# One ordered TensorE stretch per expert in a routed mixture of experts, with the row scatter split between weight tiles

## The chip, the cores and the metric

The kernel runs on one core of a Trainium2 chip. The metric is the device time of one execution in microseconds (us), as the median of several executions. Profiled numbers come from one execution recorded by the hardware profiler. Its span runs from the first to the last recorded instruction, and its own time is a little longer than the span.

## The reference

The reference is one encoder layer on 256 tokens of width 1024: an input projection, three token mixers (latent attention, a state-space scan, a convolution module), gates and an output projection, a layer norm, then a mixture of experts and a second layer norm. The change lies in the mixture of experts alone:

```
logits = t @ router_w + router_b
top_vals, top_idx = top_k(logits, 4)          # 4 of 32 experts per token
gates = softmax(top_vals)
for each expert e, for its tokens x:
    h = x @ w_gu[e] + b_gu[e]                 # 1024 -> 2048
    gate, up = min(h[:, :1024], 7), clip(h[:, 1024:], -7, 7)
    y = ((up + 1) * gate * sigmoid(1.702 * gate)) @ w_dn[e] + b_dn[e]
    out[tokens] += gates * y
x = layernorm(2 ** 0.25 * x + out)
```

All matrices are float32. The weights of one expert are 12.6 MB, those of all experts 402.7 MB, and each is read from HBM once.

## The kernel before

The mixer part comes first and takes some 400 us. The rest of the time is a loop over the 32 experts, written out in full.

**Weights.** Each expert has 12 tiles of 1 MB: 8 of the up projection (one for each 128 rows of the input width) and 4 of the down projection. They go through a ring of 19 tiles (`load`, line 721). SyncE issues the transfers in order, and each waits until TensorE has read the tile that was in that place 19 loads before. The first 19 tiles are loaded while the mixers still run.

**Two forms of an expert.** How many tokens an expert has is known only at run time. A form with 64 token slots (`many`) runs when the expert has more than 32 tokens, and a form with 32 slots (`four`) when it has at most 32, or more than 64; with more than 64 tokens (`over`) both run, and the second form takes the tokens from 65 on. Each piece is a conditional block: `on(cond, pe_part, other_part)` on line 1179 puts the first part under a branch on TensorE's queue and the second under a branch on ScalarE's and VectorE's queues. The flags come from memory into registers (line 1171). Where a block isn't taken, the queue jumps over it and raises the block's semaphores in its place. In the profiled execution 19 experts run `four` alone, 10 run `many` alone and 3 run both (counted from the matmuls of lines 1217 and 1227 in the table below).

**An expert** (`expert`, line 1168):
- `gather_more` (line 1195) for `over` alone: 32 small matmuls fetch the further tokens, into PSUM bank 1, and ScalarE and VectorE copy them out.
- The up projection in four pairs of weight tiles (`up_many`, `up_four`, lines 1210 and 1220), the `many` block and the `four` block of each pair one after the other.
- `swiglu_into` (line 1084) on VectorE and ScalarE.
- `turn_many` and `turn_four` (lines 1249 and 1263): matmuls of one column that bring the tokens' gates into slot order (`gate_mm`), for `many` also a broadcast of the expert's row of token ranks (`pbr`), the bias of the down projection, and transposes of the activations. Then VectorE copies the gates to SBUF (`gsl`, lines 1258 and 1272), builds the 0/1 scatter matrix `sc` from the ranks (`slots`, line 1099), and ScalarE copies the transposes to `hT`.
- The down projection (lines 1278 and 1286), and `weigh` (line 1141): ScalarE and VectorE multiply by the gates and split the result in two terms, `yh` and `yl`.
- For `over`, a scatter of the first form's rows into the sum (`pom`, line 1296).
- For `four`, a second broadcast of the ranks into `pb2` (line 1298), `slots` and `weigh`.

**Two pieces belong to the neighbours.** `flush(prev)` (line 1156) scatters the previous expert's rows: for each half `c` of the 256 tokens, four matmuls into two PSUM banks, then two VectorE adds into the sum `acc` (its tile bears the name `xn` in the profile). `fill` (line 1390) prepares the tokens of the next pair of experts: in an even expert it gathers them (8 matmuls of 512 columns, `pgx`, then two copies), in an odd expert it transposes them (`spread_rows`, line 973: 8 transposes, `pgt`, then 8 copies that ScalarE and VectorE take in turn from the same two banks). In the code `first` and `second` stand after the first pair of up tiles and after the activation.

**What sets the order.** The tile framework orders the instructions of each engine by a simulation, except inside `tc.manual_schedule`, which keeps the order of the code for the engines that it names. Here `pe_order()` (line 1312) encloses each piece by itself, so that the framework may place the pieces of TensorE against each other. In the trace it places both `flush` and `fill` between two experts: after an expert's last matmul of the down projection come the skipped blocks, `pbs` (that is `pb2`), then `pgt` and `pos` (`fill`, `flush`) or `pos` and `pgx`, and only then the next expert's bias and up projection.

**PSUM** has 8 banks: five fixed ones, `bank(0)` to `bank(4)`, and three that rotate under the name `sm`, which `flush`, `fill`, the gates, the ranks and `pom` share.

At the last expert (line 1404) `flush` comes ahead of a branch over a large block for experts with more than 96 tokens, which isn't taken.

Of the kernel before, what the change touches and what calls it, by code (L numbers as in the profile page):

```python
# [18 lines left out]
P = 128  # L19
# [158 lines left out]
def tile_trunk(ctx, tc, xT_d, xn_d, wf_d, vec_d, row_d, rw_d, cst_d, cst2_d, rope_d, ln1_d, ln2_d,  # L178
# [895 lines left out]
    def sm(name, shape=None):  # L1074
        return pse.tile(shape or [P, 512], F32, tag="sm", name=name, bufs=3)
# [16 lines left out]
    def gate_mm(pgs, lhs, e):  # L1092
        for c in range(2):
            l = lhs(c).bitcast(F32)
            n = l.shape[-1]
            for h in range(P // n):
                T.matmul(pgs[h * n:(h + 1) * n, 0:1], l, Gm[c][:, e:e + 1], start=(c == 0), stop=(c == 1))
# [27 lines left out]
    def gate_slots(lhs, e, name):  # L1125
# [6 lines left out]
        gsl = ex.tile([P, 1], F32, tag="gsl", name=f"gsl{name}", bufs=4)  # L1132
# [23 lines left out]
    def flush(prev):  # L1156
        if prev:
            e, sc, yh, yl = prev
            for c in range(2):
# [8 lines left out]
    def expert(e, oh, xg, bl, wt, prev, cur, fill):  # L1168
# [8 lines left out]
        first, second = (fill, lambda: flush(prev)) if e % 2 else (lambda: flush(prev), fill)  # L1177

        def on(cond, *parts):

            for c_, f in zip(cond, parts):
                if f:
                    with tc.If(c_):  # L1183
                        with pe_order():
                            f()
# [7 lines left out]
        pg = bank(1, f"pgs{e}", [P, KT, TINY])  # L1193
# [36 lines left out]
        for k0 in range(0, KT, 2):  # L1230
            on(many, lambda: up_many(k0))
            on(four, lambda: up_four(k0))
            if k0 == 0:
                with pe_order():
                    first()
# [4 lines left out]
        with pe_order():  # L1240
            second()
        pY = [bank(i, f"pY{e}{i}") for i in range(2)]
        pgL, pgS, pbr = [sm(f"pgs{e}{i}") for i in range(3)]
# [3 lines left out]
        gsl = [ex.tile([P, 1], F32, tag="gsl", name=f"gsl{e}{i}", bufs=4) for i in range(2)]  # L1247

        def turn_many():
            gate_mm(pgL, lambda c: oh[:, c, e % 2], e)  # L1250
            T.matmul(pbr[:, 0:S], idr[:, e:e + 1].to_broadcast([P, P]), rankT, start=True, stop=True)
# [5 lines left out]
        def turned_many():  # L1257
            V.tensor_copy(gsl[0], pgL[:, 0:1])
            slots(sc, pbr, 0, e)
# [3 lines left out]
        def turn_four():  # L1263
            gate_mm(pgS, lambda c: ohs[:, c], e)
# [6 lines left out]
        def turned_four():  # L1271
            V.tensor_copy(gsl[1], pgS[:, 0:1])
# [20 lines left out]
        on(many, None, lambda: weigh(pY[0], gsl[0], yh, yl))  # L1293
        for c in range(2):
            pos = [sm(f"pom{e}{c}{n}") for n in range(2)]
            on(over, lambda: scatter(pos, c, sc, (yh, yl)), lambda: [add(c, n, pos[n]) for n in range(2)])
        pb2 = sm(f"pbs{e}", [P, S])
        on(four, lambda: T.matmul(pb2, idr[:, e:e + 1].to_broadcast([P, P]), rankT, start=True, stop=True),  # L1298
           lambda: (slots(sc, pb2, 1, e), weigh(pY[1], gsl[1], yh, yl)))
# [79 lines left out]
    for e in range(NE):  # L1379
# [35 lines left out]
        expert(e, oh, xg, bl, wt, prev, cur, fill)  # L1415
        prev = cur

    with tc.manual_schedule():
# [5 lines left out]
        def total(c):  # L1424

            for n in range(2):
                pz[c][n] = bank(4, "pz11") if c and n else sm(f"pz{c}{n}")
# [142 lines left out]
```

## Time and profile before

| | |
|---|---|
| median of 3 runs | 1499.05 us (1496.07 to 1501.25) |
| profiled execution, its own time | 1502.31 us |
| its span | 1500.5 us |
| TensorE matmuls busy | 1194.4 us, 80% of the span |
| VectorE, ScalarE, GpSimd busy | 616.0, 327.5, 293.9 us |
| moved by DMA | 456.59 MB, mean 304 GB/s |
| mean granted clock of TensorE | 0.88 of full speed |
| matmul records of line 1217 (`many`, up) | 832, 64 for an expert: 13 experts |
| matmul records of line 1227 (`four`, up) | 1408, 64 for an expert: 22 experts |

The page of the profile gives busy times of engines, but a busy share is a mean over stages with different limits. How long one stage takes is read from views of a stretch: windows (busy time, granted clock and share of the DMA engines), waits (an engine and line, what it waited for, the total, how often, the longest) and timelines (start, duration, line, what is written from what, and in brackets the idle time before it and what ended that). `PEq`, `ACTq` and `DVEq` are the queues' own instructions: branches, register loads and semaphores. A float32 matmul shows as two records.

### The profile page before, as it was taken

The page shows a single profiled execution, that of the slowest core. Times are in us where ns is not written, and L with a number is a line of the kernel's source. Part 1 is how long each engine was busy: PE and PEld are TensorE (multiplying, and loading weights), DVE is VectorE, ACT ScalarE, POOL GpSimd, SP SyncE. Part 2 cuts the span into 40 slices and gives each one's busy share as a digit, 9 for nine tenths or more (in the row PEclk, how much of TensorE's full clock was granted, in tenths as well). Part 3 has the DMA queues.
Part 4 walks back from the last instruction along what each step waited for, and adds up shares of the span by engine and source line. Part 5 has one row for each costly group of instructions (what it writes and reads, how often), then busy time and mean ns, then how long its engine had stood idle before and what let it go on. Part 6 is the DMA issues. An engine that isn't in the chain of part 4 may idle for free. (4 is left out here: it accounts for less than half of the span.)

```text
span 1500.5 us, 22214 instructions
## 1 busy us (share of the span) xinstructions
PE 1194.4 (80%) x7326; PEld 626.5 (42%) x7326; DVE 616.0 (41%) x1249; ACT 327.5 (22%) x668; POOL 293.9 (20%) x293
## 2 busy tenths in 40 slices
PE   7798796999577987887788779888877788777856
PEld 7786686899424232222232224333222222222213
DVE  5999996876722232122321221323212312232203
ACT  5565563554301011011110110111101101111001
POOL 5999998432300000000000000000000000000000
PEclk9998797999795988999898897989989899988877
DMA  7343343477588779999999898687899999999850
GB/s 235 107 154 110 108 142 114 167 254 279 222 320 354 301 278 384 415 392 385 416 417 404 359 414 352 248 330 295 334 372 412 416 416 416 413 415 416 343 234 29
DMA packets 89516, 456.59 MB, mean 304 GB/s; under 512 B 8305, under 2 KB 8705, under 8 KB 58497
## 3 DMA queue, kind: packets, MB, share of 16 engines
q1 hardware_dynamic: 89344, 454.33, 77.1%
q8 instruction: 104, 1.70, 0.5%
q14 instruction: 68, 0.55, 0.1%
HBM read 453.25 MB, written 1.05 MB: 303 GB/s over the span
## 5 line engine op out<-in xcount | busy, mean ns | idle before, releaser
L1459 POOL TENSOR_TENSOR xn<-xn,lb 128x256 f32<-128x256 f32 x4 | 2.8, 718 | 1081.2 <-DVE xn L1447 1081.2
L1217 PE MATMUL pGL<-ew,xg 128*64 128x512 f32 x832 | 198.0, 619 | 10.2 <-PEq L1183 9.5
L1227 PE MATMUL pGS<-ew,xsm 128*32 128x512 f32 x1408 | 180.4, 634 | 20.8 <-PEq L1183 20.0
L388 POOL TENSOR_TENSOR cbc<-cbc,ups 128x256 f32<-128x256 f32 x120 | 119.5, 996 | 4.6
L1217 PEld LDWEIGHTS pGL<-ew,xg 128*64 128x64 f32 x832 | 59.2, 142 | 143.6 <-issue 133.1
L243 DVE TENSOR_TENSOR wl<-raw,wh 128x1024 fp32r<-128x1024 f32 (+1 forms) x72 | 99.2, 1388 | 37.3 <-ACT wh L242 37.1
L1227 PEld LDWEIGHTS pGS<-ew,xsm 128*32 128x32 f32 x1408 | 46.5, 117 | 156.7 <-issue 146.4
L1282 PE MATMUL pY<-ew,hT 128*64 128x512 f32 x416 | 99.7, 622 | 10.4 <-ACT hT L1261 4.9
L1308 PE MATMUL pY<-ew,hT 128*32 128x512 f32 x704 | 90.2, 631 | 21.3 <-PEq L1183 11.0
L1150 PE MATMUL pos<-yh,sc 64*128 64x512 f32 x124 | 66.4, 622 | 51.1 <-DVE xg L969 16.5
L387 POOL TENSOR_TENSOR ups<-ups,vec 128x256 f32<-128x256 f32 x120 | 104.5, 890 | 0.0
L242 ACT CAST wh<-raw 128x1024 fp32r<-128x1024 f32 (+1 forms) x89 | 90.9, 1029 | 57.9 <-DMA raw<-in_wf_dram 30.5
L1086 DVE TENSOR_SCALAR gv<-pGL 128x256 f32<-128x256 f32 x26 | 11.0, 424 | 221.8 <-PE pGL L1217 220.5
L1154 DVE TENSOR_TENSOR xn<-xn,pos 128x512 f32<-128x512 f32 x124 | 79.7, 684 | 25.8 <-PE pos L1150 25.4
L1087 ACT ACTIVATE sg<-gv 128x256 f32<-128x256 f32 x48 | 20.0, 417 | 305.0 <-DVE gv L1086 304.1
L1143 DVE SCALAR_TENSOR_TENSOR yl<-pY,gsl,yh 128x512 fp32r<-128x512 f32 x35 | 26.1, 746 | 113.7 <-ACTq L1183 84.7
L1142 ACT ACTIVATE yh<-pY,gsl 128x512 fp32r<-128x512 f32 x35 | 24.0, 687 | 218.3 <-PEq L1183 111.7
L1192 ACT COPY xsm<-xg 128x256 f32<-128x256 f32 x32 | 13.0, 405 | 223.7 <-PE pGS L1227 136.1
L1150 PEld LDWEIGHTS pos<-yh,sc 64*128 64x128 f32 x124 | 26.5, 235 | 83.3 <-DVE xn L1154 29.9
L1101 DVE TENSOR_SCALAR sc<-pbs,base,cst 128x256 fp32r<-128x256 f32 x22 | 12.0, 543 | 119.7 <-PE pbs L1298 119.7
L1282 PEld LDWEIGHTS pY<-ew,hT 128*64 128x64 f32 x416 | 32.0, 142 | 69.6 <-issue 61.6
L1150 PE MATMUL pos<-yl,sc 64*128 64x512 f32 x124 | 58.8, 611 | 0.0
(450 smaller groups left out, 2261.2 us busy)
## 6 DMA issues: line engine op xcount, KB each, us to landing
ew<-in_wgu_dram SPq DMA_DIRECT2D x241, 1024.0 KB, 15.2
ew<-in_wdn_dram SPq DMA_DIRECT2D x124, 1024.0 KB, 11.7
raw<-in_wf_dram SPq DMA_DIRECT2D x87, 512.0 KB, 3.7
ew<-in_wgu_dram SPq DMA_DIRECT2D x30, 512.0 KB, 5.8
ew<-in_wdn_dram SPq DMA_DIRECT2D x8, 512.0 KB, 6.0
xraw<-in_xT_dram SPq DMA_DIRECT2D x4, 256.0 KB, 5.9
xn<-in_xn_dram SPq DMA_DIRECT2D x2, 512.0 KB, 6.3
lnt<-in_ln_dram SPq DMA_DIRECT2D x2, 512.0 KB, 10.9
```

The source lines that it names most:

```text
L242: A.copy(h[:, b], raw[:, b])
L243: (PO if u in LOW_POOL else V).tensor_sub(l[:, b], raw[:, b], h[:, b].bitcast(F32))
L387: PO.tensor_tensor(pr, up[:, j:j + S], W("cw31", c * 31 + j).to_broadcast([P, S]), op=ALU.mult)
L388: PO.tensor_add(acc, acc, pr)
L1142: A.activation(yh, pY, AF.Copy, scale=gsl)
L1143: V.scalar_tensor_tensor(yl, pY, gsl, yh.bitcast(F32), op0=ALU.mult, op1=ALU.subtract)
L1150: T.matmul(pos[n], sc[r, c * P:(c + 1) * P], y[r], start=(start and i == 0), stop=(i == 1))
L1154: V.tensor_add(dst, dst, po)
L1217: T.matmul(pL[q][h * 64:(h + 1) * 64].rearrange("p (g n) -> p g n", g=2), xg[:, k, s_], quarter(wt[k], h, q), start=False, stop=(k == KT - 1))
L1227: T.matmul(grp(pS, g).rearrange("p (g n) -> p g n", g=2), xs_[:, k], quarter(wt[k], h, q), start=False, stop=(k == KT - 1))
L1282: T.matmul(pY[0][n * 64:(n + 1) * 64], hT[b][:, j, h * CAP:(h + 1) * CAP], wt[KT + 2 * b + h][:, j, n * 512:(n + 1) * 512], start=False, s ...
L1308: T.matmul(grp(pY, 2 * n + j), hT[:, j, g * TINY:(g + 1) * TINY], w[:, j, n * 512:(n + 1) * 512], start=(j == 1 and (b, h) == (0, 0)), sto ...
```

## The change

`sm` rotates over two banks in place of three, and the bank so freed is `bank(5)`. It takes `gather_more`'s output, and after that a tile `aux` for the broadcast ranks and the gates of both forms. These matmuls run without a condition in every expert, after the third pair of up tiles, as does one VectorE copy of both columns of gates; the gates and rank broadcasts of `turn_many` and `turn_four`, both conditional copies and `pb2` are gone. `flush` takes one half of the tokens at a time: half 0 after the first pair of up tiles, half 1 after the second. `fill` stands after the activation in even and odd experts alike. The whole of `expert` is inside one `pe_order()`, so TensorE keeps the order of the code through an expert.

```diff
     def sm(name, shape=None):
-        return pse.tile(shape or [P, 512], F32, tag="sm", name=name, bufs=3)
+        return pse.tile(shape or [P, 512], F32, tag="sm", name=name, bufs=2)
...
-    def flush(prev):
+    def flush(prev, cs=(0, 1)):
         if prev:
             e, sc, yh, yl = prev
-            for c in range(2):
+            for c in cs:
...
-        first, second = (fill, lambda: flush(prev)) if e % 2 else (lambda: flush(prev), fill)
...
                 if f:
                     with tc.If(c_):
-                        with pe_order():
-                            f()
+                        f()
...
-        pg = bank(1, f"pgs{e}", [P, KT, TINY])
+        pg = bank(5, f"pgs{e}", [P, KT, TINY])
...
             on(many, lambda: up_many(k0))
             on(four, lambda: up_four(k0))
-            if k0 == 0:
-                with pe_order():
-                    first()
+            if k0 <= 2:
+                flush(prev, (k0 // 2,))
+            elif k0 == 4:
+                aux = bank(5, f"aux{e}", [P, S + 2])
+                T.matmul(aux[:, 0:S], idr[:, e:e + 1].to_broadcast([P, P]), rankT, start=True, stop=True)
+                gate_mm(aux[:, S:S + 1], lambda c: oh[:, c, e % 2], e)
+                gate_mm(aux[:, S + 1:S + 2], lambda c: ohs[:, c], e)
+                gsl = ex.tile([P, 2], F32, tag="gsl", name=f"gsl{e}", bufs=4)
+                V.tensor_copy(gsl, aux[:, S:S + 2])
...
-        with pe_order():
-            second()
+        fill()
...
         def turn_many():
-            gate_mm(pgL, lambda c: oh[:, c, e % 2], e)
-            T.matmul(pbr[:, 0:S], idr[:, e:e + 1].to_broadcast([P, P]), rankT, start=True, stop=True)
             T.matmul(pY[0], bl, bdn_t, start=True, stop=False)
...
         def turned_many():
-            V.tensor_copy(gsl[0], pgL[:, 0:1])
-            slots(sc, pbr, 0, e)
+            slots(sc, aux, 0, e)
...
         def turn_four():
-            gate_mm(pgS, lambda c: ohs[:, c], e)
...
         def turned_four():
-            V.tensor_copy(gsl[1], pgS[:, 0:1])
             A.activation(hT[2], pTS, AF.Copy, scale=0.5)
...
-        on(many, None, lambda: weigh(pY[0], gsl[0], yh, yl))
+        on(many, None, lambda: weigh(pY[0], gsl[:, 0:1], yh, yl))
...
-        pb2 = sm(f"pbs{e}", [P, S])
-        on(four, lambda: T.matmul(pb2, idr[:, e:e + 1].to_broadcast([P, P]), rankT, start=True, stop=True),
-           lambda: (slots(sc, pb2, 1, e), weigh(pY[1], gsl[1], yh, yl)))
+        on(four, None, lambda: (slots(sc, aux, 1, e), weigh(pY[1], gsl[:, 1:2], yh, yl)))
...
-        expert(e, oh, xg, bl, wt, prev, cur, fill)
+        with pe_order():
+            expert(e, oh, xg, bl, wt, prev, cur, fill)
...
-                pz[c][n] = bank(4, "pz11") if c and n else sm(f"pz{c}{n}")
+                pz[c][n] = bank(4 + n, f"pz{c}{n}") if c else sm(f"pz{c}{n}")
```

## Rows read from the trace of the kernel before

**Rows 1.** Windows of stages: busy us (count) of PE, PEld, DVE, ACT, POOL; PEclk, DMA, GB/s

```profile
480.00:1110.00 630.00, 515.44 (x2900) 189.45 (x2900) 161.46 (x389) 67.06 (x152) 0.00 (x0) 0.89 0.88 354
1110.00:1400.00 290.00, 223.34 (x1404) 77.70 (x1405) 77.60 (x183) 31.79 (x69) 0.00 (x0) 0.90 1.02 415
1400.00:1437.60 37.60, 31.42 (x126) 10.32 (x124) 8.31 (x18) 2.47 (x6) 0.00 (x0) 0.86 0.85 344
```

**Rows 2.** Waits of SyncE's DMA queue, 419 to 1400 us: total, times, longest

```profile
SPq L727 <- PE pGS L1227: 223.2, 31, 23.4
```

**Rows 3.** Waits of TensorE, 450 to 1480 us: engine, line and cause; total us, times, longest

```profile
PE pos L1150 <- DVE xg L969: 16.5, 15, 2.7
PE pgt L977 <- PEq L1183: 16.4, 11, 2.7
PE pTS L1269 <- DVE gsl L1272: 16.1, 19, 1.3
PE pbs L1298 <- PEq L1183: 16.0, 18, 1.1
PE pos L1150 <- PEq L1183: 15.3, 12, 2.6
PE pos L1150 <- DVE xn L1154: 14.0, 30, 2.2
PE pGS L1223 <- PEq L1183: 12.4, 17, 0.8
...
PE pTL L1255 <- DVE uv L1090: 6.7, 10, 0.7
...
PE pgs L1199 <- DVE yl L1143: 4.2, 3, 1.4
PE pom L1150 <- DVE xn L1154: 3.7, 3, 1.2
PE pos L1150 <- DVE sc L1101: 2.8, 2, 1.4
...
PE pGS L1227 <- DMA ew<-in_wgu_dram: 0.8, 2, 0.4
```

**Rows 4.** Timelines of TensorE: a pair of up tiles, a down bias, the 8 transposes of `spread_rows`

```profile
1174.70 1.92 PE L1227 MATMUL pGS<-ew,xsm 128*32 128x512 f32 x16 [0.45 <-PEq L1183]
...
1181.89 1.05 PE L1266 MATMUL pY<-bdn_t,bl 128*32 128x512 f32 x4
...
1371.79 1.06 PE L977 MATMUL pgt<-cst,rawx 128*128 128x128 f32 x8 [0.82 <-PEq L1183]
```

**Rows 5.** Timeline of VectorE, 1187 to 1200 us: last copy of `spread_rows`, adds of `flush`

```profile
1194.21 0.41 DVE L969 TENSOR_SCALAR xg<-pgt,lgb 128x128 f32<-128x128 f32 x1 [0.18 <-ACT xg L971]
1194.92 1.29 DVE L1154 TENSOR_TENSOR xn<-xn,pos 128x512 f32<-128x512 f32 x2 [0.31 <-PE pos L1150]
```

**Rows 6.** Timeline of ScalarE, 1187 to 1200 us: first copy of `spread_rows`

```profile
1191.93 0.46 ACT L971 ACTIVATE xg<-pgt,lgb 128x128 f32<-128x128 f32 x1 [1.92 <-PE pgt L977]
```

**Rows 7.** Timeline of VectorE, 1209 to 1214 us: first and last of the activation's operations

```profile
1209.68 0.42 DVE L1086 TENSOR_SCALAR gv<-pGS 128x256 f32<-128x256 f32 x1 [0.20 <-DVE ohp L955]
...
1211.13 0.42 DVE L1090 SCALAR_TENSOR_TENSOR uv<-uv,gv 128x256 f32<-128x256 f32 x1
```

**Rows 8.** Groups of TensorE's instructions, 450 to 1480 us: the gates

```profile
L1097 PE MATMUL pgs<-Gm,ohs 128*32 128x1 f32 x336 | 6.8, 176 | 7.0 <-PEq L1183 5.8 <-DVEq L1183 1.2
L1097 PE MATMUL pgs<-Gm,ohp 128*64 128x1 f32 x104 | 5.2, 201 | 3.3 <-PEq L1183 2.9 <-ACT sg L1087 0.4
```

**Rows 9.** Queue instructions of line 1171: engine, count, ns min/median/max, first and last

```profile
L1171 PEldq TENSOR_LOAD <-flag x96: 297/303/490, 398.1 to 1450.9; - x96
```

**Rows 10.** Windows between changes of the granted clock, columns as in rows 1

```profile
450.00:1450.00 1000.00, 792.40 (x4531) 289.66 (x4532) 257.72 (x613) 105.11 (x236) 0.00 (x0) 0.87 0.92 373
...
1167.20:1170.60 3.40, 3.27 (x8) 2.17 (x7) 0.69 (x2) 0.28 (x1) 0.00 (x0) 0.51 1.01 419
...
1191.10:1201.40 10.30, 8.76 (x36) 3.83 (x39) 4.30 (x9) 1.72 (x4) 0.00 (x0) 0.50 1.02 414
```

More of the change, by code (lines that the diff above doesn't have):

```diff
@@ L1096, in gate_mm @@
             for h in range(P // n):
-                T.matmul(pgs[h * n:(h + 1) * n, 0:1], l, Gm[c][:, e:e + 1], start=(c == 0), stop=(c == 1))
+                T.matmul(pgs[h * n:(h + 1) * n], l, Gm[c][:, e:e + 1], start=(c == 0), stop=(c == 1))
     def slots(sc, pbr, slot_, e):
@@ L1131, in gate_slots @@
                 T.matmul(pgs[h * n:(h + 1) * n], l, Gm[c][:, e:e + 1], start=(c == 0), stop=(c == 1))
-        gsl = ex.tile([P, 1], F32, tag="gsl", name=f"gsl{name}", bufs=4)
+        gsl = ex.tile([P, 2], F32, tag="gsl", name=f"gsl{name}", bufs=4)[:, 0:1]
         V.tensor_copy(gsl, pgs)
@@ L1239, in expert @@
         on(four, None, lambda: swiglu_into(uv[2], pS))
-        with pe_order():
-            second()
+        fill()
         pY = [bank(i, f"pY{e}{i}") for i in range(2)]
-        pgL, pgS, pbr = [sm(f"pgs{e}{i}") for i in range(3)]
         pTL = bank(2, f"pTL{e}", [P, 2, 2, P])
@@ L1246, in expert @@
         hT = [ex.tile([P, 2, P], F32, tag="hT", name=f"hT{e}{i}", bufs=4) for i in range(3)]
-        gsl = [ex.tile([P, 1], F32, tag="gsl", name=f"gsl{e}{i}", bufs=4) for i in range(2)]
         def turn_many():
-            gate_mm(pgL, lambda c: oh[:, c, e % 2], e)
-            T.matmul(pbr[:, 0:S], idr[:, e:e + 1].to_broadcast([P, P]), rankT, start=True, stop=True)
             T.matmul(pY[0], bl, bdn_t, start=True, stop=False)
```

## The prediction

> **What bounds it now.** I read the windows of the expert stages first. From 480 to 1110 us the DMA engines are at 0.88 of their time, and from 1110 to 1400 us at 1.02, moving 415 GB/s, which is all they give [rows 1]. That looks like a kernel bound by its weights. The waits correct it: the `four` up projections waited 0.8 us in all for weight tiles between 450 and 1480 us [rows 3], while the queue that issues the weights waited 223.2 us for the `four` matmuls to free a place in the ring, in one row of several [rows 2]. So TensorE sets the pace, the transfers follow it, and in the last 290 us both are close to their limits. TensorE itself is busy 792.4 of 1000 us [rows 10], and its idle time, split by cause [rows 3], is the ledger from which I work. The third thing to see is the granted clock: 0.87 in the mean from 450 to 1450 us [rows 10], that is, TensorE was at 1.2 GHz in place of 2.4 GHz in 26% of that time.
>
> **How far a gain can reach.** Of the 384 weight tiles 365 pass through the ring in the stage; at 415 GB/s one of 1.049 MB takes 2.53 us, and an expert's twelve take 30.3 us. The DMA engines were idle for 0.12 x 630 = 76 us and for 0.15 x 37.6 = 6 us [rows 1]. No more than about 82 us can go, whatever TensorE gains.
>
> **Part 1, waits that go** [rows 3]. All are idle time on the chain.
> - The gates' copy ahead of the transposes, 16.1 us. It stood behind the activation on VectorE; now it comes before the fourth pair of up tiles. What the transposes still need, the activation, ends 1.87 us after its first operation starts [rows 7], and `fill` now lies there: a gather that takes TensorE 3.27 us [rows 10], or eight transposes of 1.06 us and a down bias of 1.05 us [rows 4]. Without that cover, 1.87 us would be open in each expert.
> - The activation ahead of the `many` transposes, 6.7 us over ten experts; the last two have no `fill` and keep it, so 5.4 us.
> - `flush` waiting for banks that `spread_rows` or its own adds still hold, 16.5 and 14.0 us. Each half now has a pair of up tiles behind it, 1.92 us and a skipped block of 0.45 us [rows 4], against 1.29 us for two adds [rows 5].
> - `gather_more` waiting for `weigh` to leave bank 1 (4.2 us), and `flush` waiting for the second scatter matrix of an `over` expert (2.8 us).
> - The other way, `pom`: 3.7 us for three experts with three banks [rows 3]. With two, the second half waits for both adds, 1.29 us and their start, some 1.9 us in place of 1.2 us each: 2 us more.
>
> Together 16.1 + 5.4 + 30.5 + 7.0 - 2 = 57 us.
>
> **Part 2, what is added.**
> - Both forms' gates in every expert. The 13 `many` sets took 5.2 us and the 21 `four` sets 6.8 us [rows 8], so 0.40 and 0.32 us each: 19 x 0.40 + 10 x 0.32 = 11 us, among the up tiles and covered by nothing. The rank broadcast is made 32 times in place of 35, which is worth nothing.
> - `spread_rows` in the 15 odd experts that have one. It used to lie between two experts. Its copies take 1194.62 - 1191.93 = 2.69 us [rows 5, 6], ScalarE and VectorE in turn, and in the new place they queue behind the activation's 1.87 us [rows 7]. The copy to `hT`, for which the down projection waits, queues behind them on ScalarE: 4.56 us after the activation starts. TensorE has 1.06 + 1.05 us of its own in that time and a skipped block of 0.45 us [rows 4]; that leaves 2.0 us, and less with the first copy (0.46 us) beside the activation and the two transposes still to come. I take 1.3 us, 15 x 1.3 = 19 us. The bounds: 0, if the framework puts the `hT` copy ahead, and 2.69 us each, 40 us. Who waits: the down projection, and behind it the release of four ring tiles.
> - The boundary of two experts. Before, its idle time ended by queue instructions was 16.0 + 16.4 + 15.3 + 12.4 = 60 us [rows 3], some 1.9 us an expert: skipped blocks and flags. The block of `pb2` goes, but the three flag loads, 0.30 us each [rows 9], now stand in a row at the head of the expert, where nothing hides them. `weigh` no longer counts there: its result is wanted only after the next expert's first up tiles. I take 0. The bounds are 14 us less (one skipped block of 0.45 us in each of 31 [rows 4]) and 19 us more (two flag loads that lay beside matmuls, 0.6 us in each).
>
> So the idle time falls by 57 - 11 - 19 = 27 us.
>
> **Part 3, the clock.** This is the largest term that the waits don't show. The clock fell after the thin stretch of an expert's end: down matmuls, skipped blocks, one broadcast, transposes, `flush` with its waits. After a spread it stayed at 1.2 GHz for 10.3 us, in which TensorE was busy 8.76 us; after a gather for 3.4 us [rows 10]. Work at 1.2 GHz takes twice as long, so the difference of 6.9 us costs 6.9 x 0.85 / 2 = 2.9 us. In the new order the spread doesn't stand at the boundary; the next bias and up tiles follow at once. Along the timeline ten of the 15 spreads precede an expert of `four`; if each of these boundaries becomes like one after a gather, that is 29 us, and I take 30. The bounds: 0, if the spread's new place or the boundary alone keeps the clock down as long, and 260 x 0.85 / 2 = 110 us, if no slow stretch were left.
>
> **Part 4, weights that come late.** In the stretch where the DMA engines are at 1.02 TensorE's gain can turn into waits for tiles. Its share of 57 us is 290 of 1000 us, 16 us. The ring is refilled in each `many` expert, which takes longer than 30.3 us, so I take 3 us of it; bounds 0 and 16.
>
> **Sum.** -27 - 30 + 3 = -54 us. The profiled execution took 1502.3 us (span 1500.5 us), which gives 1448 us; the median of the runs is 3.3 us below that execution, so 1445 us. The end of the kernel (the branch over the large block, the last expert, the layer norm) isn't touched.
>
> **A rule against the change.** The rows say that the missing bank costs 2 us, in `pom`, because adds of 1.29 us fit beside 1.92 us of up tiles [rows 4, 5]. The Trainium skill, page "Perfetto Trace Analysis", section "Identifying Performance Opportunities", says that the same gap recurring on the engine that should be saturated can mean that PSUM or SBUF has no room for the next tile. By that rule, taking a bank from a shared pool should make such gaps longer, and the sum would be that of the second rival. The trace agrees so far as 14.0 us of gaps of this kind are there with three banks [rows 3].
>
> **Rivals.**
> 1. The clock gives nothing back. For it: the boundary keeps its 1.9 us of branches and flags and now has no matmul in it at all. Against it: dense up tiles follow at once. 1445 + 30 = 1475 us.
> 2. Two banks are too few: half 1 of `flush` waits for both adds of half 0 in each of the 30 experts that contain one. The 14.0 us don't go and 30 x 1.29 = 39 us come: 1445 + 53 = 1498 us, no change. For it: VectorE may have other work in front of the adds. Against it: it is busy 77.60 of 290 us [rows 1].
> 3. Slower: the `hT` copy in the odd experts. If the whole 4.56 us lie open, with TensorE's own work ahead of them and not beside them, that is 68 us in place of 19, and a gap of that size takes the clock's 30 us with it: 1445 + 49 + 30 = 1524 us. It decides from 2.9 us of wait in each odd expert: 1.6 us x 15 = 24 us and the 30 us are then the whole gain. For it: both engines must finish the copies in turn. Against it: 2.0 us were left by the rows.
> 4. More than forecast: the `hT` copy is placed early (-19 us) and most of the clock comes back (-30 us more). 1396 us by that sum, but the transfers stop it at about 82 us: 1417 us.
>
> **How the numbers follow.** My sum 0.52, rival 1 0.17, rival 2 0.07, rival 3 0.12, rival 4 0.12. A measurement of this kernel can tell about 0.3% (4.5 us) from no change. Faster: 0.52 + 0.17 + 0.12 = 0.81; the same: 0.07; slower: 0.12. The range reaches from 1405 us (rival 4 with its own margin) to 1500 us (rival 2 included); it leaves out rival 3 and a little beyond rival 4.
>
> **What would show it.** Right: no wait of `pTS` for `gsl` and hardly one of `pos` for `xn` or `xg`; matmuls of `pos` between blocks of `pGS` or `pGL`; a granted clock above 0.90; a DMA share above 0.92 from 480 to 1110 us; a new row of `pY` waiting for `hT` near 20 us in the odd experts. Wrong: that row above 43 us (rival 3), `pos` waiting for `xn` above 14 us (rival 2), a granted clock still at 0.87 (rival 1), or TensorE waiting for `ew` by more than 16 us.

## The result, and the profile after

The changed kernel takes 1411.76 us (median; 1410.67 to 1423.35) against 1500.15 us for the kernel before on the same chip: a ratio of 0.9428, 95% interval 0.9372 to 0.9484. The forecast was 1445 us with a range of 1405 to 1500. So the side was right and the gain of 88 us was larger than the 54 us of the sum; it came out near rival 4 (1417 us), which had 0.12. The profiled execution took 1411.15 us, span 1409.3 us.

The simplest ledger is the first part of the page: TensorE's busy time, and the span less it. The page of the changed kernel (busy us, share of the span, count; then the granted clock and the DMA engines' share in tenths, in 40 slices of the span):

```profile
PE 1142.4 (81%) x7635; PEld 598.0 (42%) x7635; DVE 618.7 (44%) x1246; ACT 326.4 (23%) x668; POOL 292.7 (21%) x293
...
PEclk9898888999969999999999998999999999998988
...
DMA  7342343467949979999999999998999999999980
```

The span fell by 1500.5 - 1409.3 = 91.2 us. TensorE was busy 1194.4 us and is busy 1142.4 us, 52 us less, though it has 309 more matmul records. The other 39 us are idle time. A busy time that falls while the work grows points to the clock, and the windows show that most of it is. Windows of the changed kernel (columns as in [rows 1]):

```profile
450.00:1350.00 900.00, 734.79 (x4779) 259.39 (x4775) 252.56 (x596) 103.12 (x237) 0.00 (x0) 0.94 0.99 399
480.00:1110.00 630.00, 524.47 (x3456) 187.22 (x3456) 184.86 (x437) 74.21 (x170) 0.00 (x0) 0.95 0.99 398
1110.00:1330.00 220.00, 169.46 (x1101) 56.55 (x1093) 57.86 (x135) 22.30 (x51) 0.00 (x0) 0.92 1.02 415
```

Against [rows 1, 10] the granted clock of the expert stage went from 0.87 to 0.94: 26% of 1000 us at 1.2 GHz became 12% of 900 us, 260 us against 108. The two stretches are not the same share of the work; from 400 us to the end the windows give 0.87 of 1100.5 us and 0.92 of 1009.3 us, so about 286 us at 1.2 GHz against 161. The DMA engines, which were at 0.88 from 480 to 1110 us, are at 0.99.

The idle time, from the waits of TensorE from 420 to 1390 us in the changed kernel (columns as in [rows 3]; all rows of this view together are 184 us, those of the kernel before from 420 to 1481 us 217 us):

```profile
PE pGS L1221 <- PEq L1182: 56.4, 18, 3.5
...
PE pGL L1211 <- PEq L1182: 13.3, 5, 3.0
PE pGS L1225 <- DMA ew<-in_wgu_dram: 11.1, 16, 1.4
PE pY L1302 <- ACT hT L1269: 9.9, 18, 0.6
...
PE pGL L1211 <- PEq L1403: 6.9, 1, 6.9
...
PE pY L1302 <- DMA ew<-in_wdn_dram: 5.6, 4, 1.4
...
PE pTL L1254 <- DVE uv L1090: 3.7, 5, 1.1
...
PE pos L1150 <- DVE xn L1154: 0.7, 1, 0.7
```

Of the waits of [rows 3], `pTS` for `gsl` and `pos` for `xg` are gone, and `pos` for `xn` is down from 14.0 to 0.7 us. The first row is where the remaining idle time now stands together: the bias matmuls at the head of an expert of `four`, 3.1 us each.

### The profile page after: what moved, and what is told of

It is laid out like the page before. It is cut to its first block, busy times and chain, and to the rows that moved or that the text cites. A ratio compares the mean times of both kernels' runs of the same rounds, so it can differ in the third digit from the quotient of the medians.

```text
span 1409.3 us, 21939 instructions
## 1 busy us (share of the span) xinstructions
PE 1142.4 (81%) x7635; PEld 598.0 (42%) x7635; DVE 618.7 (44%) x1246; ACT 326.4 (23%) x668; POOL 292.7 (21%) x293
## 3 DMA queue, kind: packets, MB, share of 16 engines
HBM read 453.25 MB, written 1.05 MB: 322 GB/s over the span
## 5 line engine op out<-in xcount | busy, mean ns | idle before, releaser
L1225 PE MATMUL pGS<-ew,xsm 128*32 128x512 f32 x1408 | 185.3, 639 | 35.0 <-PEq L1182 19.5
L1215 PE MATMUL pGL<-ew,xg 128*64 128x512 f32 x832 | 206.8, 642 | 0.9 <-PEq L1182 0.9
L1302 PE MATMUL pY<-ew,hT 128*32 128x512 f32 x704 | 86.9, 608 | 23.8 <-ACT hT L1269 9.9
L1278 PE MATMUL pY<-ew,hT 128*64 128x512 f32 x416 | 95.0, 598 | 9.8 <-ACT hT L1259 5.4
L1221 PE MATMUL pGS<-bgu_t,bl 128*32 128x512 f32 x176 | 33.9, 847 | 63.7 <-PEq L1182 56.4
L1302 PEld LDWEIGHTS pY<-ew,hT 128*32 128x32 f32 x704 | 20.2, 110 | 77.4 <-issue 43.1
L243 POOL TENSOR_TENSOR wl<-raw,wh 128x1024 fp32r<-128x1024 f32 x17 | 41.9, 2468 | 51.1 <-ACT wh L242 39.7
L1101 DVE TENSOR_SCALAR sc<-aux,base,cst 128x256 fp32r<-128x256 f32 x22 | 11.9, 543 | 83.4 <-PEq L1182 83.4
L1221 PEld LDWEIGHTS pGS<-bgu_t,bl 128*32 128x32 f32 x176 | 4.6, 123 | 81.8 <-issue 52.3
```

Source lines behind the costliest of these rows:

```text
L243: (PO if u in LOW_POOL else V).tensor_sub(l[:, b], raw[:, b], h[:, b].bitcast(F32))
L1215: T.matmul(pL[q][h * 64:(h + 1) * 64].rearrange("p (g n) -> p g n", g=2), xg[:, k, s_], quarter(wt[k], h, q), start=False, stop=(k == KT - 1))
L1221: T.matmul(grp(pS, g), bl[:, g * TINY:(g + 1) * TINY].bitcast(F32), bgu_t[:, q * 512:(q + 1) * 512].bitcast(F32), start=True, stop=False)
L1225: T.matmul(grp(pS, g).rearrange("p (g n) -> p g n", g=2), xs_[:, k], quarter(wt[k], h, q), start=False, stop=(k == KT - 1))
L1278: T.matmul(pY[0][n * 64:(n + 1) * 64], hT[b][:, j, h * CAP:(h + 1) * CAP], wt[KT + 2 * b + h][:, j, n * 512:(n + 1) * 512], start=False, s ...
L1302: T.matmul(grp(pY, 2 * n + j), hT[:, j, g * TINY:(g + 1) * TINY], w[:, j, n * 512:(n + 1) * 512], start=(j == 1 and (b, h) == (0, 0)), sto ...
```

## The experiments

All idle and busy figures in the table come from the page of each kernel (span, and TensorE's busy time). The ratio is to the kernel before on the same chip, where its median lay between 1499.03 and 1501.71 us; what gates_alone, order_alone and fewer_before cost or save is told from it.

| kernel | median us | ratio, 95% interval | span | TensorE busy | idle |
|---|---|---|---|---|---|
| before | 1500.15 | 1 | 1500.5 | 1194.4 | 306.1 |
| changed | 1411.76 | 0.9428, 0.9372 to 0.9484 | 1409.3 | 1142.4 | 266.9 |
| gates_alone | 1529.86 | 1.0196, 1.0172 to 1.0221 | 1530.8 | 1239.5 | 291.3 |
| order_alone | 1493.65 | 0.9962, 0.9946 to 0.9979 | 1491.4 | 1175.0 | 316.4 |
| gates_conditional | 1417.94 | 0.9440, 0.9398 to 0.9483 | 1414.4 | 1143.0 | 271.4 |
| flush_whole | 1446.56 | 0.9646, 0.9591 to 0.9701 | 1439.2 | 1154.2 | 285.0 |
| flush_at_head | 1484.32 | 0.9895, 0.9863 to 0.9928 | 1482.5 | 1200.4 | 282.1 |
| fill_at_head | 1423.00 | 0.9506, 0.9464 to 0.9547 | 1419.3 | 1138.0 | 281.3 |
| both_at_head | 1554.01 | 1.0341, 1.0297 to 1.0385 | 1553.6 | 1230.0 | 323.6 |
| fewer_before | 1496.84 | 0.9986, 0.9973 to 0.9999 | 1499.7 | 1195.8 | 303.9 |
| fewer_after | 1401.82 | 0.9333, 0.9303 to 0.9364 | 1401.5 | 1146.5 | 255.0 |
| flags_early | 1404.22 | 0.9366, 0.9318 to 0.9413 | 1394.6 | 1129.8 | 264.8 |
| flags_after_fill | 1400.18 | 0.9337, 0.9303 to 0.9371 | 1397.3 | 1132.6 | 264.7 |
| flags_and_one_over | 1396.21 | 0.9316, 0.9279 to 0.9353 | 1394.1 | 1131.4 | 262.7 |

### Do the weights bind, before or after?

The last weight tile of each expert from the second on isn't loaded, and the tile before it is used in its place, in both kernels. TensorE's work stays, a twelfth of the transfers goes.

```diff
-        wt = [load(e, u) for u in range(12)]
+        wt = [load(e, u) for u in range(12 if e == 0 else 11)]
+        wt += wt[10:11] * (12 - len(wt))
```

> The same removal of one tile of twelve in the kernel before. If TensorE paced it and the transfers only followed, as the prediction said, the time stays within 5 us of 1500 us. If the full DMA engines of the last 290 us held it, 15 us or more go.

> The changed kernel without the last of the twelve weight tiles of each expert from the second on: the tile before it is read in its place, so TensorE does the same work and 31 of 365 transfers of the stage (78 us at 415 GB/s) fall away. If the changed kernel is paced by TensorE and only lost the 18.5 us of waits for weights that its trace shows, near its end, about 8 to 18 us go: 1395 to 1404 us. If the transfers paced it altogether, up to 78 us go, near 1340 us. If the weights never mattered, it stays within 4 us of 1412 us.

The kernel before gains 2 us in 1500, the changed kernel 10 us by the medians and 14 by the ratios. TensorE set the pace in the first, as the prediction said, and still does in most of the second. What the transfers take back in the changed kernel is 10 to 14 us, beside 18.5 us of waits for `ew` in its trace (11.1 + 5.6 and two small rows), which are 1.0 us in fewer_after.

### One half of the change at a time

The gates and ranks in the bank `aux` behind the third pair of up tiles, with `sm` at two banks, in the kernel before, whose order the framework still sets:

```diff
-        return pse.tile(shape or [P, 512], F32, tag="sm", name=name, bufs=3)
+        return pse.tile(shape or [P, 512], F32, tag="sm", name=name, bufs=2)
...
+            elif k0 == 4:
+                with pe_order():
+                    aux = bank(5, f"aux{e}", [P, S + 2])
...
```

> The kernel before with the gates and ranks in one bank without conditions (and two banks in the shared pool) and nothing else of the change: the framework still places the pieces of TensorE. Theory (the place and order of the scatter and the fill bring the gain): the 16.1 us of waits for the gates' copy and some 7 us of bank 1 and of the second scatter matrix go, 11 us of gates come, and two banks make the scatter's waits longer: 1485 to 1500 us. Rival (the gates bring the gain): 1450 us or less.

And the whole expert in one ordered stretch, with `first` and `second` where they stand in the code, the old gates and three banks:

```diff
-                    with tc.If(c_):
-                        with pe_order():
-                            f()
+                    with tc.If(c_):
+                        f()
...
-        expert(e, oh, xg, bl, wt, prev, cur, fill)
+        with pe_order():
+            expert(e, oh, xg, bl, wt, prev, cur, fill)
```

> The kernel before with the whole expert in one ordered stretch and nothing else of the change: the scatter or the fill after the first pair of up tiles, the other after the activation, conditional gates, three banks. Theory: the single gather matmul that held the first expert for 13.5 us is gone, nothing is left between two experts, and the clock recovers: 1425 to 1450 us. Rival (the gates bring the gain): 1475 us or more.

Both missed. The gates alone cost 30 us, the order alone saves 6, and the two together with the split and the new places of `flush` and `fill` save 88: the parts can't be added. The ledger tells why the gates alone lose. Idle time falls by 15 us, but TensorE is busy 45 us longer, of which the added gate matmuls are about 16 (their two groups are busy 28.3 us here and 12.3 us in the kernel before). The granted clock from 400 us to the end is 0.85, against 0.87. The timeline shows where the framework put them (TensorE of gates_alone; start, duration, line, output from inputs, idle time before and its releaser):

```profile
1190.50 0.51 PE L1150 MATMUL pos<-yh,sc 64*128 64x512 f32 x2 [1.67 <-ACTq L1183]
...
1191.71 0.40 PE L1097 MATMUL aux<-Gm,ohp 128*64 128x1 f32 x8
...
1194.18 1.39 PE L963 MATMUL pgx<-nh,ohp 128*128 128x512 f32 x2 [0.60 <-DVE xn L1154]
1195.37 1.05 PE L963 MATMUL pgx<-nl,ohp 128*128 128x512 f32 x2
```

They too went to the boundary, among the matmuls of `flush`, and the gather behind them runs at the low clock (0.52 from 1194 to 1196 us): 1.05 us for two records that take 0.63 us in the changed kernel. Which of the three edits in this run (banks, place, one copy) cost what wasn't separated.

In order_alone the waits of TensorE (420 to 1480 us) show that the places in the code were not good ones yet:

```profile
PE pos L1150 <- DVE xn L1154: 35.4, 31, 2.1
...
PE pgs L1097 <- DVEq L1183: 21.5, 19, 1.4
```

A whole `flush` waits for its own adds in every expert, in odd experts behind the activation that VectorE is busy with (2.1 us), and the old gates wait in 19 experts.

### Where `flush` and `fill` stand

Four kernels change nothing but these places in the changed kernel. `flush` whole behind the first pair of up tiles:

```diff
-            if k0 <= 2:
-                flush(prev, (k0 // 2,))
+            if k0 == 0:
+                flush(prev)
```

> The changed kernel with both halves of the scatter after the first pair of up tiles. Theory (the split pays for the missing bank): with two banks the second half waits for both adds of the first, some 1.5 to 2 us in each of 30 experts, so a wait of pos for xn of 45 to 60 us appears and the time grows by 25 to 50 us, to 1437 to 1462 us. Rival (two banks are enough as they are, the split is worth nothing): within 5 us of 1412 us.

Both at the head of the expert, ahead of the up tiles, in the order of the kernel before (`fill` first in odd experts, `flush` first in even ones):

```diff
         on(over, gather_more, copy_more)
+        if e % 2:
+            fill()
+        flush(prev)
+        if e and e % 2 == 0:
+            fill()
...
-            if k0 <= 2:
-                flush(prev, (k0 // 2,))
-            elif k0 == 4:
+            if k0 == 4:
...
-        fill()
+        if e == 0:
+            fill()
```

> The changed kernel with the scatter (whole) and the fill at the head of each expert, ahead of its up projection, as the framework had placed them before; all else as changed. Theory (the place brings the gain, through waits and through the granted clock): the flush waits, the open wait for the activation (1.9 us less the 1.4 us of bias and skipped block) and the slow clock at the boundary come back: 1480 to 1530 us, clock 0.88 or lower. Rival (a fixed order and the gates bring it, wherever the pieces stand): under 1440 us.

`fill` alone at the head, `flush` split as in the changed kernel (the edit above without its lines on `flush`); and `flush` alone at the head, whole, with `fill` after the activation (without its lines on `fill`):

> Changed kernel, but the gather or spread (fill) stands at the head of each expert, ahead of its up tiles; flush stays split behind the first two up pairs. With the runs already made the four arrangements of these two steps are then complete (both inside 1412 us, flush whole 1447, flush whole and fill at the head 1554). Theory (the place of fill is the larger term, for it covers the activation ahead of the transposes and leaves no thin stretch at the boundary): the transposes pTS and pTL wait for uv again, 1.9 us and 0.7 us an expert, about 35 us; spread at the boundary waits for its own copies; granted clock from 480 to 1110 us below 0.92; in all 70 to 110 us more than the changed kernel, 1480 to 1520 us. Rival (flush is the larger term, and once it is split fill may stand anywhere): less than 35 us more, below 1447 us, clock still 0.94 or more.

> Changed kernel, but flush stands whole at the head of each expert, ahead of its up tiles; fill stays after the activation. Runs already made: flush split inside and fill at the head 1423 us, flush whole behind the first up pair and fill inside 1447, both at the head 1554. Theory (flush is the term, by itself: at the head its second half waits for the adds of the first and nothing dense lies between, so that the clock falls): 1480 to 1540 us, pos waiting for xn about 30 us, granted clock from 480 to 1110 us at 0.90 or below. Rival (the two steps cost much only where they meet at the boundary, because they pass the two shared banks back and forth there): 1445 to 1465 us, as behind the first up pair, with the clock at 0.93 or more.

both_at_head came out 24 us above its range, so the two steps together cost more than expected. For `fill` alone the theory fell and the rival held: 11 us, not 70 to 110. (The four runs are not the complete square that this expectation calls them, since flush_whole has `flush` behind the first pair; flush_at_head was run for the missing corner.) The waits of the transposes for the activation did come back, 17.2 + 10.2 us, but idle time rose by only 14 us in all, and the clock stayed at 0.95. For `flush` the theory held: 73 us, near the lower edge of its range, with 28.1 us of `pos` waiting for `xn` and a clock of 0.89 from 480 to 1110 us. This edit does two things, since `flush` at the head is whole: 35 us are there already with `flush` whole behind the first pair (flush_whole), and the place costs the other 38 us.

With `flush` split inside, moving `fill` costs 11 us; with `flush` at the head it costs 70 us (1554 - 1484). With `fill` inside, moving `flush` to the head costs 73 us; with `fill` at the head, 131 us. So `flush` is the larger term, and 58 us of the 142 are there only when both stand at the boundary.

What a moved `flush` costs is mostly not a wait. From the table, flush_at_head has 15 us more idle time than the changed kernel (the 28.1 us of waits for `xn` come, 15.5 us of waits for `ew` go) and is busy 58 us longer, with the same matmuls. By tile, from 400 us on, `pos` is busy 82.7 us in place of 46.9, and `pGL` and `pGS`, the bias and up tiles behind it, 456.0 us in place of 434.4. Its windows and its timeline across one boundary:

```profile
450.00:1350.00 900.00, 736.13 (x4463) 258.91 (x4461) 239.11 (x571) 96.48 (x223) 0.00 (x0) 0.88 0.94 376
```

```profile
1117.10 1.92 PE L1301 MATMUL pY<-ew,hT 128*32 128x512 f32 x16 [0.46 <-PEq L1182]
1121.45 0.51 PE L1150 MATMUL pos<-yh,sc 64*128 64x512 f32 x2 [2.43 <-PEq L1182]
1121.75 0.44 PE L1150 MATMUL pos<-yl,sc 64*128 64x512 f32 x2
1122.93 1.39 PE L1150 MATMUL pos<-yh,sc 64*128 64x512 f32 x2 [0.74 <-DVE xn L1154]
1123.53 1.22 PE L1150 MATMUL pos<-yl,sc 64*128 64x512 f32 x2
1125.06 1.93 PE L1222 MATMUL pGS<-bgu_t,bl 128*32 128x512 f32 x8 [0.32 <-PEq L1182]
```

Two boundaries of the changed kernel, the second at the same place:

```profile
1084.53 1.93 PE L1221 MATMUL pGS<-bgu_t,bl 128*32 128x512 f32 x8 [2.96 <-PEq L1182]
1086.21 2.43 PE L1225 MATMUL pGS<-ew,xsm 128*32 128x512 f32 x16
...
1104.66 1.92 PE L1302 MATMUL pY<-ew,hT 128*32 128x512 f32 x16 [0.46 <-PEq L1182]
1109.65 1.06 PE L1221 MATMUL pGS<-bgu_t,bl 128*32 128x512 f32 x8 [3.07 <-PEq L1182]
1110.51 1.93 PE L1225 MATMUL pGS<-ew,xsm 128*32 128x512 f32 x16
1112.36 0.50 PE L1150 MATMUL pos<-yh,sc 64*128 64x512 f32 x2
...
1113.55 1.92 PE L1225 MATMUL pGS<-ew,xsm 128*32 128x512 f32 x16 [0.46 <-PEq L1182]
1115.40 0.50 PE L1150 MATMUL pos<-yh,sc 64*128 64x512 f32 x2
...
1123.15 1.05 PE L1263 MATMUL pY<-bdn_t,bl 128*32 128x512 f32 x4 [0.32 <-PEq L1182]
1124.13 0.44 PE L1266 MATMUL pTS<-cst,uv 128*128 128x128 f32 x2
1125.13 1.92 PE L1302 MATMUL pY<-ew,hT 128*32 128x512 f32 x16 [0.56 <-ACT hT L1269]
```

Read the durations, not the gaps. In the first kernel a gap of 2.43 us, little work and a second gap of 0.74 us are followed by the second half of `flush` and a bias at half speed, and the windows show a granted clock of 0.50 for 6.80 us (1122.8 to 1129.6). In the changed kernel a single longer gap of 3.07 us is followed by a bias of 1.06 us at full speed, but at the boundary before it a gap of 2.96 us is followed by a bias of 1.93 us, with a clock of 0.50 for 3.40 us (1083.9 to 1087.3). So the single gap doesn't keep the clock up: of the 22 biases of `four`, 12 are slow (over 1.7 us) in the changed kernel and 19 in flush_at_head. What differs is how long the clock stays down, about 161 us in all from 400 us on (0.92 of 1009.3) against 281 us (0.87 of 1082.5), and what runs meanwhile: the halves of `flush` in the changed kernel stand between up tiles with no idle time ahead of them, at full speed. The gap at the boundary didn't go; what went is the thin work and the second gap behind it. Why one gap of 3 us lowers the clock and the next one doesn't stays open.

flush_whole lies between: `flush` stands behind dense tiles and the clock holds (0.95 from 450 to 1350 us), but its second half waits for the adds of the first:

```profile
PE pos L1150 <- DVE xn L1154: 23.7, 31, 0.8
```

The time is in the range of the expectation, the wait only half of the 45 to 60 us there. Of the 30 us by which its span is longer, 18 are idle and 12 are busy time, with the clock no lower (0.93 from 400 us on, against 0.92): `pos` is busy 61.9 us in place of 46.9. The timeline shows how: held back one behind the other, the two records of the second half overlap less than those of the first, at a granted clock of 1.00.

```profile
1121.59 0.50 PE L1150 MATMUL pos<-yh,sc 64*128 64x512 f32 x2
...
1123.11 1.09 PE L1150 MATMUL pos<-yh,sc 64*128 64x512 f32 x2 [0.78 <-DVE xn L1154]
```

So a longer busy time is not the clock alone.

That wait is the rule weighed in the prediction. Three banks gave 14.0 us of this wait before [rows 3]; two banks and a whole `flush` give 23.7 us; two banks and a split one 0.7 us. The Trainium skill, page "Perfetto Trace Analysis", section "Identifying Performance Opportunities", says that recurring gaps on the engine that should be full can mean too little room in PSUM or SBUF. The trace agrees with it for a whole `flush`; for the split one other work takes the place of the bank.

### The gates' conditions

The gates' matmuls and copies back under the two conditions, ahead of the transposes; banks, order and the rank broadcast as changed:

```diff
-                gate_mm(aux[:, S:S + 1], lambda c: oh[:, c, e % 2], e)
-                gate_mm(aux[:, S + 1:S + 2], lambda c: ohs[:, c], e)
...
-                V.tensor_copy(gsl, aux[:, S:S + 2])
...
         def turn_many():
+            gate_mm(aux[:, S:S + 1], lambda c: oh[:, c, e % 2], e)
...
         def turn_four():
+            gate_mm(aux[:, S + 1:S + 2], lambda c: ohs[:, c], e)
```

> The changed kernel with the gates' matmuls and their copies back under the conditions, ahead of the transposes; the broadcast of the ranks stays without condition. Theory: 11 us of matmuls go, but the copy stands behind the activation (and in odd experts behind the copies of the fill) again and the transposes wait for it, 0.5 to 1.5 us in each expert: 1412 to 1435 us. Rival (the early gates are the main part): 1450 us or more.

The median is 6 us longer, and the intervals overlap. In the changed order the gates' conditions are worth little. The transposes' wait for the copy, on which the expectation rests, isn't in the trace; the gates' matmuls wait instead, 11.9 us in 11 experts (`aux`, ended by `DVEq`).

### What is left at the boundary

TensorE's three flag loads of the next expert, moved from the head of that expert to the place behind the gates' matmuls (flags_early), or to the place behind `fill` (flags_after_fill):

```diff
+                if e + 1 < NE:
+                    pe_flags[e + 1] = flags(e + 1, (ENG.PE,))
```

> The changed kernel with TensorE's three flag loads of the next expert after the third pair of up tiles in place of the head of that expert. They are 0.30 us each and stand in a row in the 3.0 us that TensorE idles between two experts. Theory (the flags are 0.9 us of that, and the transfers leave some 10 us of gain): the idle time at the boundary falls to about 2.1 us, TensorE waits longer for weights, and the time falls by 5 to 15 us, to 1397 to 1407 us. Rival (the transfers already set the pace): within 4 us of 1412 us. Second rival (TensorE alone sets it): 28 us less, 1384 us.

> Changed kernel, but TensorE's three flag loads of the next expert stand right after fill, ahead of the transposes, in place of the head of the next expert. Theory (the loads are hidden where matmuls of several us are queued ahead of them): idle time at the boundary falls from 3.0 to about 1.9 us and does not come back in even experts, behind a gather of 3.3 us, and only in part in odd ones, behind eight transposes of 1.06 us; weights then set the pace, and the time lies between 1393 and 1403 us. Rival (the loads cost TensorE 0.9 us wherever they stand, as they did behind the gates' matmuls): a new idle time of about 1.4 us ahead of the transposes or of the bias before them in every expert, and a time of 1402 to 1412 us.

And, on top of the second, `pom`, the scatter of an `over` expert (the middle form), as one conditional block in place of two, its second half in banks 2 and 3:

```diff
-        for c in range(2):
-            pos = [sm(f"pom{e}{c}{n}") for n in range(2)]
-            on(over, lambda: scatter(pos, c, sc, (yh, yl)), lambda: [add(c, n, pos[n]) for n in range(2)])
+        pos = [[sm(f"pom{e}0{n}") for n in range(2)], [bank(2 + n, f"pom{e}1{n}") for n in range(2)]]
+        on(over, lambda: [scatter(pos[c], c, sc, (yh, yl)) for c in range(2)],
+           lambda: [add(c, n, pos[c][n]) for c in range(2) for n in range(2)])
```

> As flags_after_fill, and the scatter of an expert of the middle form is one conditional block in place of two, its second half in the banks of the up projection: one skipped block fewer on TensorE at each boundary. Theory (transfers set the pace by now): idle time at the boundary falls by another 0.4 us to about 1.5 us, waits of the up and down projections for weight tiles grow by about as much, and the time is within 4 us of flags_after_fill. Rival (TensorE still sets the pace): 29 blocks of 0.4 us, 8 to 12 us less than flags_after_fill, and no more waits for weight tiles.

Behind the gates' matmuls the loads take 1.2 us from the boundary and put as much back ahead of the fourth pair of up tiles, as the timeline of flags_early has it:

```profile
1092.85 1.06 PE L1225 MATMUL pGS<-bgu_t,bl 128*32 128x512 f32 x8 [1.86 <-PEq L1186]
...
1104.34 1.92 PE L1229 MATMUL pGS<-ew,xsm 128*32 128x512 f32 x16 [1.50 <-PEq L1186]
```

So of its theory the shorter boundary came true; the longer waits for weights didn't (18.6 us of `ew`, against 18.5). The time is in its range, but its interval overlaps that of the changed kernel.

Behind `fill` little comes back: the idle time ahead of the down biases grows from 6.8 to 9.8 us over all experts, the transposes follow the bias without idle time, and the idle time of the boundary turns into waits for weights. Timelines of flags_after_fill, then of flags_and_one_over:

```profile
1106.33 1.09 PE L977 MATMUL pgt<-cst,rawx 128*128 128x128 f32 x8
1107.74 1.05 PE L1269 MATMUL pY<-bdn_t,bl 128*32 128x512 f32 x4 [0.32 <-PEq L1186]
...
1116.13 1.61 PE L1309 MATMUL pY<-ew,hT 128*32 128x512 f32 x8 [2.82 <-DMA ew<-in_wdn_dram]
```

```profile
1085.70 1.93 PE L1225 MATMUL pGS<-bgu_t,bl 128*32 128x512 f32 x8 [1.51 <-ACTq L1186]
...
1093.16 1.07 PE L1229 MATMUL pGS<-ew,xsm 128*32 128x512 f32 x8 [1.20 <-DMA ew<-in_wgu_dram]
```

The waits and the windows of flags_and_one_over show the end of this road:

```profile
PE pGS L1229 <- DMA ew<-in_wgu_dram: 43.5, 44, 2.5
...
PE pY L1309 <- DMA ew<-in_wdn_dram: 11.8, 11, 2.0
```

```profile
480.00:1110.00 630.00, 526.02 (x3575) 181.31 (x3569) 189.15 (x453) 76.96 (x177) 0.00 (x0) 0.97 1.01 409
```

Waits for `ew` are 61.2 us here with the small rows, 52.2 us in flags_after_fill and 18.5 us in the changed kernel, and the DMA engines are at 1.01. The theory of both runs held as far as these rows go: weights set the pace from here. No run took transfers away from these two kernels, so that part is read from waits and shares. Their idle time in all is only 2 to 4 us below that of the changed kernel; the busy time is 10 to 11 us shorter, at a clock of 0.94 from 400 us on against 0.92. flags_and_one_over, at 1396.21 us, beats both kernels; its interval ends below the one of the changed kernel begins. Against flags_after_fill its 4 us can't be told from nothing.

## Why the prediction was right on the side and short on the size

**What bounds it.** Right. Without a twelfth of the transfers the kernel before gains 2 us. The limit on a gain, 82 us of idle transfer time, was too low: the changed kernel gained 88 us, and flags_and_one_over 103 us by its ratio. The sum began at 480 us and left out the start of the stage, where the DMA engines of the kernel before stood at 0.05 from 400 to 420 us, 19 us idle; in the changed kernel, whose first expert starts earlier, they are at 0.43 there.

**Part 1, waits that go: 57 us forecast, 50 measured.** The rows named there made 65.1 us from 420 to 1481 us, and what answers to them in the changed kernel makes 15.2 us. The copy of the gates and both waits of `flush` went as said. `fill` covers the activation in all but the 3.7 us of `pTL`; the gather takes 2.1 us there and not 3.27, since the window of [rows 10] shows it at half speed, and that still covers 1.87 us. Not seen: the wait of `gather_more` didn't go but grew from 4.2 to 6.2 us, 4.1 of it for `sc`. By the kernel's code its new bank, `bank(5)`, is the one that holds `aux`, which `slots` of the expert before reads late to write `sc`; no run tested that. `pom` was forecast at 2 us more and has 1.1 us less.

**Part 2, what is added.**
- The gates of both forms: 11 us forecast. Their groups are busy 12.4 + 9.5 us against 12.0 us before [rows 8], so 10 us. Right.
- `spread_rows` ahead of the `hT` copy: 19 us forecast, none measured. The lower bound was right. ScalarE in an odd expert of the changed kernel:

```profile
1122.41 0.42 ACT L1087 ACTIVATE sg<-gv 128x256 f32<-128x256 f32 x1 [14.53 <-DVE gv L1086]
1122.74 0.44 ACT L971 ACTIVATE xg<-pgt,lgb 128x128 f32<-128x128 f32 x1
1124.69 0.38 ACT L1269 ACTIVATE hT<-pTS 128x256 f32<-128x256 f32 x1 [1.51 <-PEq L1182]
1124.97 1.39 ACT L971 ACTIVATE xg<-pgt,lgb 128x128 f32<-128x128 f32 x3
```

  Only one of its four copies stands ahead of `hT`, three behind. The step that failed is "The copy to `hT`, for which the down projection waits, queues behind them on ScalarE": the order is kept on TensorE alone, and the framework sets that of ScalarE. The down projection waits 0.56 us there, and 0.53 us in an even expert.
- The boundary: 0 forecast between -14 and +19. The idle time ahead of an expert's first matmuls was 67 us (from 420 to 1481 us, causes as in the prediction) and is 81 us, so +15, near the upper end. The flag loads are the reason the prediction gave for that end, and flags_early shows them: 3.07 us become 1.86 us without them.

**Part 3, the clock: 30 us forecast, 50 to 60 measured.** This term was mis-sized by nearly a factor of two. TensorE is busy 52 us less with 10 us more of gates, so 62 us. The windows give (286 - 161) us at 1.2 GHz from 400 us to the end, busy for 0.8 of it, half of that lost, 50 us, and by the two stretches of 1000 and 900 us (260 - 108) x 0.8 / 2 = 61 us. By tile, from 400 us on, it is the moved pieces that are busy for less time: `pos` 81.7 us before and 46.9 us after, `pgx` 54.9 and 33.5, `pgt` 21.9 and 16.5, 62 us in all. Part of that is not the clock, as flush_whole shows for `pos`. The up tiles run no faster (`pGL` and `pGS` together 417.8 us before, 434.4 us after). The reasoning by [rows 10] took only the boundaries after a spread as curable and those after a gather as the floor. The experiments turn that around: `fill` at the boundary hardly costs any clock by itself (busy 1138.0 us, no more than the 1142.4 us of the changed kernel), and `flush` whole there costs 58 us of busy time.

**Part 4, late weights: 3 us forecast, 17 measured,** a little beyond the upper bound of 16. The 18.5 us of waits for `ew` are over the 16 us that the prediction named as a sign of being wrong, and for this term it was. They came from the gains above: TensorE ran up to the transfers and waited there, and 10 to 14 us come back when a twelfth of them goes.

**Not forecast.** Two gains that lie outside the steps. The branch at the last expert leaves TensorE idle for 6.9 us in place of the 11.9 us before. And the first expert starts earlier. The framework had put one matmul of the gather for the next pair ahead of the first expert's bias, and it waited 13.5 us for a one-hot matrix, so that the bias started at 414.70 us. With the expert in one ordered stretch it starts at 404.06 us, and 5 us of that are left at the second expert, which starts at 433.52 in place of 438.49 us.

**Together.** Idle time from 420 us on: -50 for the waits of part 1, -4 for the down projection, +15 for the boundary, +17 for the weights, -5 for the branch, -6 for skipped blocks and flags ahead of other matmuls, in all -33 us. With the start of the stage -39, and -52 busy, this is the 91 us. The idle part came out near its forecast (-35 us without the gates) by terms that offset each other, which is luck in part; the gain beyond the forecast is busy time, most of it the clock.

**The rivals.** Rival 1 and rival 3 fell by the clock of 0.94 and by the `hT` row. Rival 2 is right for a whole `flush`: its wait is 23.7 us in flush_whole, where 39 us were worked out. Rival 4 is nearest to what happened, and both of its reasons came true: the `hT` copy came early and the clock came back by more. Its stop did not: the transfers held back 10 to 14 us of the changed kernel (fewer_after), and three later kernels are faster than 1417 us by 13 to 21 us.

## What to carry to other kernels

Count idle time and busy time of the bounding engine apart, and set the granted clock beside the second: more than half of the gain here was busy time, and 58 of the 73 us that a badly placed step cost. It is not the clock alone, since matmuls that wait for each other also show a longer busy time. Put short work that waits for another engine between dense pieces, half at a time, and not at the boundary where a gap already stands; a missing buffer is then made up for by the work between, as it was here. Pieces of such a change don't add up: each half alone gave -6 or +30 us, the whole change -88, so they must be judged in the order in which they end up.

## What the runs showed of the hardware

- A gap of about 3 us ahead of dense tiles was followed by full speed at one boundary (3.07 us, a bias of 1.06 us) and by half speed at the one before it (2.96 us, a bias of 1.93 us, a clock of 0.50 for 3.40 us). With a short `flush` between gaps of 2.43 and 0.74 us the clock was 0.50 for 6.80 us.
- At a granted clock of 1.00 the second half of a whole `flush` shows 1.09 us for two records that take 0.50 us where nothing holds the second one back (flush_whole): busy time of matmuls also grows with waits between them.
- Three flag loads into registers, 0.30 us each, cost TensorE 1.2 us where its queue had nothing else, 1.15 us behind 24 small matmuls (the idle time there went from 0.35 to 1.50 us), and behind a gather or eight transposes 3 us in all over the experts.
- The transfers reached 1.01 of the DMA engines' time at 409 GB/s from 480 to 1110 us. From the changed kernel to flags_after_fill the idle time ahead of an expert's first matmuls fell from 81 to 47 us, and the waits for tiles rose from 18.5 to 52.2 us.
